# Whole 1 MB weight pieces split at once, from one pool of five tiles, and a narrow expert's product in three steps

## The chip, the cores and the metric

The kernel runs on one core of one Trainium2 chip. The metric is the device time of one execution in microseconds (us). TensorE is called PE, VectorE DVE, ScalarE ACT, GpSimd POOL and SyncE SP. An engine works through its own instructions in the order in which the program holds them, and waits where another engine's result, or a buffer, is not there yet.

## The reference

A trunk of two layers on 256 tokens of 1,024 channels, in float32:

```python
# layer 0: multi-head latent attention, then a dense SwiGLU of 3584 hidden channels
x = x + mla_mixer(rmsnorm(x, norm_mix[0]), ...)
h = rmsnorm(x, norm_ffn[0])
x = x + (silu(h @ ffn_w_gate) * (h @ ffn_w_up)) @ ffn_w_down
# layer 1: mLSTM, then the best 2 of 8 experts, each a SwiGLU of 3584 hidden channels
x = x + mlstm_mixer(rmsnorm(x, norm_mix[1]), ...)
h = rmsnorm(x, norm_ffn[1])
logits = h @ router; top_v, top_i = top_k(logits, 2); gates = softmax(top_v)
for e in range(8):
    y = y + combine[..., e:e+1] * ((silu(h @ wg[e]) * (h @ wu[e])) @ wd[e])
x = rmsnorm(x + y, final_norm)
```

The result must be as exact as float32. PE multiplies rounded numbers, so the kernel takes each weight as a sum of two rounded parts.

## The kernel before

**Weights.** They come by DMA from SP's queue in pieces of 1 MB, 128 partitions by 2,048 columns, into a pool of 10 slots (`raw`). `split` makes the two parts of a piece: ACT writes `whi`, the rounded copy (L204), and DVE writes `wlo`, what is left (L208). It does this in two halves of 1,024 columns, with four tiles for `whi` and four for `wlo`. A raw slot is free once DVE has read it, and a tile once PE has.

**FFN** (112 to 340 us). Seven chunks of 512 hidden channels, six pieces each: two of the gate, two of the up and two of the down weights.

**mLSTM** (340 to 460 us). `by_channel(0)` and `by_channel(1)` make queries and keys, two pieces each; `by_token` makes the values and the output gate. Between them stand small steps on DVE: the reciprocal root `mix1` (L378), the gates, and `convolved`, whose first step copies the query sums out of their PSUM bank times `rb` (`qks`, L898). `rb` comes out of `mix1`. PSUM has four banks with the tag "a": the two `by_channel` take all of them, and `by_token` gets its two when the `qks` of `by_channel(0)` have been done.

**Chores.** The router's logits are partly made by dot products of 1,024 columns on DVE (L768). They lie in the list `chores`: 64 of `out_dot` (8 rows of `mlstm_w_out` times 8 experts) and later 16 of `x_dot`. Each call of `split` takes one from the list and issues it ahead of its own split, from the third chunk of the FFN on. What is left when a stage ends is issued in one go:

```python
        if chores and begun[0]:
            chores.pop(0)()
...
    while chores:
        chores.pop(0)()
    aT = x_mix.pair
```

**Experts** (460 to 1436 us). Eight experts, each of seven chunks of six pieces. Wide and narrow ones alternate. A wide one has 128 slots for tokens, and a piece takes 12 matmuls of 512 columns there. A narrow one has 64, its two parts stand side by side in one operand, and a piece takes 8. In a narrow chunk `both_parts` turns the chunk's gate and up values by 16 small matmuls (L1307) and makes the product at once: ACT's silu (L1310), DVE's product (L1311), ACT's rounded part (L1312), DVE's rest (L1313). `Stream.run` sets the order: it keeps `AHEAD` halves split ahead of the one that PE takes, and `soon(n, f)` issues f after n more halves. The numbers `T_LAG`, `T_LAST` and `LAST` say how many halves `both_parts` waits and where the last expert's end begins.

Of the kernel before, what the change touches and what calls it, by code (L numbers as in the profile page):

```python
# [69 lines left out]
def trunk(ctx: ExitStack, tc: tile.TileContext, out, rope_inv, x, positions, norm_mix, norm_ffn,  # L70
# [71 lines left out]
    class Stream:  # L142
# [43 lines left out]

    def split(v, sub=nc.vector):
        vs = v if isinstance(v, list) else [v]
        shape = [P, 2, 512] if isinstance(v, list) else list(v.shape)
        n = int(np.prod(shape[1:]))  # L190
        hi = weights.tile([P, 1024], F32R, name=uniq("whi"), tag="whi", bufs=NB_HI)[:, :n]
        lo = weights.tile([P, 1024], F32R, name=uniq("wlo"), tag="wlo", bufs=NB_LO)[:, :n]
        if len(shape) == 3:
            hi = hi.rearrange("p (k c) -> p k c", k=shape[1])
            lo = lo.rearrange("p (k c) -> p k c", k=shape[1])
        if chores and begun[0]:
            chores.pop(0)()
        with ExitStack() as order:
            if held:
                for ins in held.pop(0):  # L200
                    order.enter_context(tc.issue_after(ins))
            for i, part in enumerate(vs):
                h, l = (hi[:, i], lo[:, i]) if isinstance(v, list) else (hi, lo)
# [236 lines left out]
    class Out:  # L440
# [6 lines left out]
        def weights(self, i):  # L447
            raw = load(self.w[i], [P, 2, D])
            return [split(raw[:, kk]) for kk in range(2)]

# [340 lines left out]
    class Chunk:  # L791


        def __init__(self, aT, r, nb, wg, wu, wd, c, down, before):
            self.nb, self.wd, self.c, self.down = nb, wd, c, down
            self.hid = []
            act = []
            for which, w in enumerate((wg, wu)):
                p = [ps("a", [P, 512]) for _ in range(nb)]
                for i in range(2):  # L800
                    raw = load(w[c, i], [P, 4, 512])
                    for k2 in range(2):
                        wp = split(raw[:, 2 * k2:2 * k2 + 2])
                        for b in range(nb):
                            k = 4 * i + 2 * k2
                            mm3s([(p[b], tok(aT, k + kk, b), at(wp, slice(None), kk), k + kk == 0, k + kk == KB - 1)
                                  for kk in range(2)])
# [24 lines left out]
        def finish(self, i):  # L832
            raw = load(self.wd[2 * self.c + i], [P, 2, D])
            self.down(self.c, i, self.parts, [split(raw[:, kk]) for kk in range(2)])

# [47 lines left out]
    def by_channel(piece):  # L883
        p2 = [ps("a", [P, 2, S]) for _ in range(2)]
        for i in range(2):
            raw = load(mlstm_w_in[piece, i], [P, 4, 512])
            for k2 in range(2):
                wp = split(raw[:, 2 * k2:2 * k2 + 2])
                for j in range(4):
                    for kk in range(2):  # L890
                        k = 4 * i + 2 * k2 + kk
# [79 lines left out]
    def by_token(c0):  # L971
        pv = [ps("a", [P, 512]) for _ in range(NT)]
        for i in range(2):
            raw = load(mlstm_w_in[c0 // 512, i], [P, 4, 512])
            for k2 in range(2):
                wp = split(raw[:, 2 * k2:2 * k2 + 2])
                for b in range(NT):
                    for kk in range(2):
                        k = 4 * i + 2 * k2 + kk
                        mm3(pv[b], tok(aT, k, b), at(wp, slice(None), kk), k == 0, k == KB - 1)  # L980
# [276 lines left out]

    def inner(e, i, p, j, w):
        if i + j == 0:
            p.append(ps("a", [P, 512]))  # L1260
        xg = tokens[e][0]
        k = 4 * i + 2 * j
        if not WIDE[e]:
            mm2s([(p[0], xg[:, k + kk], at(w, slice(None), kk), k + kk == 0, k + kk == KB - 1) for kk in range(2)])
            return
        mm3s([(p[0], (xg[:, 0, k + kk], xg[:, 1, k + kk]), at(w, slice(None), kk), k + kk == 0, k + kk == KB - 1)
              for kk in range(2)])

    def gated(e, c, p):
# [5 lines left out]
        if c == 3 and e + 1 < NE:  # L1275
# [18 lines left out]
    def upped(e, c, p):  # L1294
# [4 lines left out]
        else:  # L1299
            nc.scalar.copy(h, p[0])  # L1300

        def both_parts():

# [5 lines left out]
            hid = tmp([P, 2, 4, N], F32, "hT_lo")  # L1309
            nc.scalar.activation(hid[:, 0], t[:, 0], AF.Silu)  # L1310
            nc.vector.tensor_mul(hid[:, 1], t[:, 1], hid[:, 0])  # L1311
            nc.scalar.copy(pair[:, :, :N], hid[:, 1])  # L1312
            nc.vector.tensor_sub(pair[:, :, N:], hid[:, 1], pair[:, :, :N].bitcast(F32))  # L1313
            hT[e, c] = pair

        def transposed():
# [4 lines left out]
            lo = tmp([P, 4, P], F32R, "hT_lo")  # L1321
            nc.scalar.copy(hi, t)
            nc.vector.tensor_sub(lo, t, hi.bitcast(F32))
            hT[e, c] = hi, lo

        moe.soon(T_LAST if (e, c) == (NE - 1, NCH - 1) else T_LAG, transposed if WIDE[e] else both_parts)

# [4 lines left out]

    def outer(e, c, i, j, w):
        k = 2 * i + j
        for h in range(2):
            if c + k == 0:
                acc[h] = ps("b", [P, 512])
        if not WIDE[e]:
            mm2s([(acc[h], hT[e, c][:, k], at(w, slice(None), slice(h * 512, h * 512 + 512)),
                   c + k == 0, c == NCH - 1 and k == 3) for h in range(2)])  # L1340
            return
        mm3s([(acc[h], at(hT[e, c], slice(None), k), at(w, slice(None), slice(h * 512, h * 512 + 512)),
               c + k == 0, c == NCH - 1 and k == 3) for h in range(2)])

# [171 lines left out]
    gather(ohs[0], first_parts, 1)  # L1516
    moe.fill(4)
    their_weights()
# [114 lines left out]
```

## Time and profile before

| | |
|---|---|
| median of 3 runs | 1442.95 us (1442.86 to 1444.77) |
| profiled execution | 1442.82 us, of which the span from the first to the last instruction is 1441.1 us |
| PE busy | 1384.9 us (96%) |
| DVE busy | 1255.8 us (87%) |
| ACT busy | 997.6 us (69%) |
| mean granted clock of PE | 0.993 of full speed |

All times are counted from the span's start. The profiled execution has 1.7 us around its span. A busy PE may be a PE that goes slowly, since matmuls are pipelined and the ends of their records are modelled; so a stage's limit is read from its waits and from the time of one chunk.

### The profile page before, as it was taken

The page shows a single profiled execution, that of the slowest core. Times are in us where ns is not written, and L with a number is a line of the kernel's source. Part 1 is how long each engine was busy: PE and PEld are TensorE (multiplying, and loading weights), DVE is VectorE, ACT ScalarE, POOL GpSimd, SP SyncE. Part 2 cuts the span into 40 slices and gives each one's busy share as a digit, 9 for nine tenths or more (in the row PEclk, how much of TensorE's full clock was granted, in tenths as well). Part 3 has the DMA queues.
Part 4 walks back from the last instruction along what each step waited for, and adds up shares of the span by engine and source line. Part 5 has one row for each costly group of instructions (what it writes and reads, how often), then busy time and mean ns, then how long its engine had stood idle before and what let it go on. Part 6 is the DMA issues. An engine that isn't in the chain of part 4 may idle for free.

```text
span 1441.1 us, 18851 instructions
## 1 busy us (share of the span) xinstructions
PE 1384.9 (96%) x6457; PEld 1080.9 (75%) x6457; DVE 1255.8 (87%) x1604; ACT 997.6 (69%) x1272; POOL 51.4 (4%) x99
## 2 busy tenths in 40 slices
PE   7999999999999899999999999999999999999995
PEld 5888888888777688766688877678886667887663
DVE  6869998857987988999998898998899899889996
ACT  5544444445854777878877788877777887778885
POOL 4300000000031000000000000000000000000000
PEclk9999999999999999999999999999999999999998
DMA  9456656555557868899999999999999999999990
GB/s 360 154 203 220 216 194 227 193 177 206 204 201 287 290 234 339 326 380 368 407 354 335 360 365 363 395 406 361 334 375 357 364 404 371 341 376 352 384 370 32
DMA packets 63614, 439.06 MB, mean 305 GB/s; under 512 B 7489, under 2 KB 7654, under 8 KB 11798
## 3 DMA queue, kind: packets, MB, share of 16 engines
q1 hardware_dynamic: 61478, 428.15, 78.5%
q0 software_dynamic: 1872, 9.61, 1.8%
q8 instruction: 52, 0.85, 0.2%
q14 instruction: 52, 0.43, 0.1%
q10 hardware_dynamic: 160, 0.02, 0.0%
HBM read 436.67 MB, written 1.08 MB: 304 GB/s over the span
## 4 chain that ended last, share of the span: by engine, by line
PE 81%; DVE 10%; issue 3%; ACT 3%; POOL 1%; DMA 0%; ACTq 0%; DVEq 0%; POOLq 0%
PE ps_a L220 10%; PE ps_a L221 10%; PE ps_a L223 10%; PE ps_a L230 8%; DVE wlo L208 6%; PE ps_a L228 6%; PE ps_b L230 4%; PE ps_b L220 3%; PE ps_b L223 3%; PE ps_b L221 3%; PE ps_a L1307 3%; PE ps_b L228 3%; PE ps_b L215 3%; PE ps_b L213 3%; PE ps_b L214 3%
## 5 line engine op out<-in xcount | busy, mean ns | idle before, releaser
L208 DVE TENSOR_TENSOR wlo<-raw,whi 128x1024 fp32r<-128x1024 f32 (+1 forms) x783 | 914.5, 1218 | 99.1 <-ACT whi L204 97.6
L204 ACT CAST whi<-raw 128x1024 fp32r<-128x1024 f32 (+1 forms) x792 | 793.2, 1048 | 200.4 <-PE ps_a L221 107.6
L220 PE MATMUL ps_a<-whi,xg 128*128 128x512 f32 x448 | 177.0, 395 | 1.1 <-ACT whi L204 1.1
L221 PE MATMUL ps_a<-whi,xg 128*128 128x512 f32 x448 | 176.5, 394 | 0.0
L230 PE MATMUL ps_a<-wlo,xg 128*128 128x512 f32 x448 | 156.1, 430 | 12.2 <-DVE wlo L208 12.2
L228 PE MATMUL ps_a<-whi,xg 128*128 128x512 f32 x448 | 142.2, 399 | 0.0
L223 PE MATMUL ps_a<-wlo,xg 128*128 128x512 f32 x448 | 140.3, 394 | 1.9 <-DVE wlo L208 1.9
L230 PEld LDWEIGHTS ps_a<-wlo,xg 128*128 128x128 f32 x448 | 72.1, 188 | 76.4 <-DVE wlo L208 70.3
L223 PEld LDWEIGHTS ps_a<-wlo,xg 128*128 128x128 f32 x448 | 83.8, 188 | 22.7 <-DVE wlo L208 3.2
L220 PEld LDWEIGHTS ps_a<-whi,xg 128*128 128x128 f32 x448 | 84.2, 188 | 20.8 <-ACT whi L204 1.5
L228 PEld LDWEIGHTS ps_a<-whi,xg 128*128 128x128 f32 x448 | 82.7, 188 | 22.5 <-ACT whi L204 4.5
L221 PEld LDWEIGHTS ps_a<-whi,xg 128*128 128x128 f32 x448 | 84.2, 188 | 19.8 <-DVE xg L1500 0.5
L220 PE MATMUL ps_b<-whi,hT_hi 128*128 128x512 f32 x224 | 91.2, 407 | 0.0
L220 PE MATMUL ps_a<-whi,xT_hi 128*128 128x512 f32 x224 | 88.6, 395 | 0.1
L221 PE MATMUL ps_a<-whi,xT_lo 128*128 128x512 f32 x224 | 88.4, 394 | 0.0
L221 PE MATMUL ps_b<-whi,hT_lo 128*128 128x512 f32 x224 | 88.3, 394 | 0.0
L768 DVE CUSTOM_DVE_ANT_0 junk<-raw,wr 128x1024 bf16<-128x1024 f32 x64 | 78.0, 1219 | 2.1 <-DMA raw<-mlstm_w_out_dram 1.6
L230 PE MATMUL ps_b<-wlo,hT_hi 128*128 128x512 f32 x224 | 76.3, 420 | 0.5 <-DVE wlo L208 0.5
L228 PE MATMUL ps_b<-whi,hT_hi 128*128 128x512 f32 x224 | 73.9, 409 | 1.0 <-ACT whi L204 1.0
L223 PE MATMUL ps_b<-wlo,hT_hi 128*128 128x512 f32 x224 | 70.3, 395 | 0.0
L223 PE MATMUL ps_a<-wlo,xT_hi 128*128 128x512 f32 x224 | 70.0, 393 | 0.0
L213 PE MATMUL ps_b<-whi,hT_hi 128*128 128x512 f32 x152 | 60.9, 401 | 0.0
(443 smaller groups left out, 1883.0 us busy)
## 6 DMA issues: line engine op xcount, KB each, us to landing
raw<-moe_w_gate_dram SPq DMA_DIRECT2D x112, 1024.0 KB, 7.1
raw<-moe_w_up_dram SPq DMA_DIRECT2D x112, 1024.0 KB, 7.0
raw<-moe_w_down_dram SPq DMA_DIRECT2D x105, 1024.0 KB, 7.3
raw<-ffn_w_gate_dram SPq DMA_DIRECT2D x14, 1024.0 KB, 5.0
raw<-ffn_w_up_dram SPq DMA_DIRECT2D x14, 1024.0 KB, 4.8
raw<-ffn_w_down_dram SPq DMA_DIRECT2D x14, 1024.0 KB, 4.8
raw<-mlstm_w_in_dram SPq DMA_DIRECT2D x12, 1024.0 KB, 5.1
raw<-mla_w_out_dram SPq DMA_DIRECT2D x4, 1024.0 KB, 7.7
```

What stands on the lines that cost most here:

```text
L204: nc.scalar.copy(h, part)
L208: sub.tensor_sub(l, part, h.bitcast(F32))
L213: nc.tensor.matmul(o, l[0], r[0], start=start, stop=False)
L214: nc.tensor.matmul(o, l[0], r[1], start=False, stop=False)
L215: nc.tensor.matmul(o, l[1], r[0], start=False, stop=stop)
L220: nc.tensor.matmul(o, l[0], r[0], start=start, stop=False)
L221: nc.tensor.matmul(o, l[1], r[0], start=False, stop=False)
L223: nc.tensor.matmul(o, l[0], r[1], start=False, stop=stop)
L228: nc.tensor.matmul(o, l, r[0], start=start, stop=False)
L230: nc.tensor.matmul(o, l, r[1], start=False, stop=stop)
L768: nc.vector.tensor_tensor_reduce(junk, a, b, 1.0, 0.0, OP.mult, OP.add, acc)
L1307: nc.tensor.matmul(t[:, n, j], src[:, j * P:(j + 1) * P], twice, start=n + j == 0, stop=n + j == 4)
```

## The change

A piece is split whole: one ACT copy and one subtraction on DVE of 2,048 columns each. Both parts come from one pool, "part", of five tiles of 2,048 columns; a split of up to 1,024 columns keeps both parts in one such tile, and the gates' weights of the mLSTM (`wg`) take a tile of it too. There are nine raw slots. `soon`, `AHEAD`, `LAST` and `T_LAG` count pieces now. The product of a narrow expert comes in three steps, one piece apart: the small matmuls, then silu and product, then the two parts. The cast and the rest of a wide expert come a piece behind their transposes. One early `fill` at the start of the experts is left out. `split` itself still takes one chore per call, but there is one call per piece where there were two.

```diff
-NB_RAW = 10
-NB_HI = 4
-NB_LO = 4
-AHEAD = 3
+NB_RAW = 9
+NB_PART = 5
+AHEAD = 2
...
-LAST = 10
-T_LAG = 2
-T_LAST = 1
+LAST = 7
+T_LAG = 1
...
-            self.items.append((partial(get, 0), lambda w: use(0, w), None))
-            self.items.append((partial(get, 1), lambda w: use(1, w), after))
+            self.items.append((lambda sub: split(load(None if key in early else src(), shape, key), sub), use, after))
...
-        hi = weights.tile([P, 1024], F32R, name=uniq("whi"), tag="whi", bufs=NB_HI)[:, :n]
-        lo = weights.tile([P, 1024], F32R, name=uniq("wlo"), tag="wlo", bufs=NB_LO)[:, :n]
+        if n <= 1024:
+            t = weights.tile([P, 2048], F32R, name=uniq("whl"), tag="part", bufs=NB_PART)
+            hi, lo = t[:, :n], t[:, 1024:1024 + n]
+        else:
+            hi, lo = (weights.tile([P, 2048], F32R, name=uniq(name), tag="part", bufs=NB_PART) for name in ("whi", "wlo"))
...
         if chores and begun[0]:
             chores.pop(0)()
...
                     raw = load(w[c, i], [P, 4, 512])
-                    for k2 in range(2):
-                        wp = split(raw[:, 2 * k2:2 * k2 + 2])
...
+                    wp = split(raw)
...
-    wg = weights.tile([P, KB, 2, 2 * HEADS], F32R, name=uniq("whi"), tag="whi", bufs=NB_HI)
+    wg = weights.tile([P, KB, 2, 2 * HEADS], F32R, name=uniq("wg"), tag="part", bufs=NB_PART)
...
+        at_end = (e, c) == (NE - 1, NCH - 1)
+
+        def then(f):
+
+            f() if at_end else moe.soon(1, f)
+
...
-            nc.scalar.activation(hid[:, 0], t[:, 0], AF.Silu)
-            nc.vector.tensor_mul(hid[:, 1], t[:, 1], hid[:, 0])
-            nc.scalar.copy(pair[:, :, :N], hid[:, 1])
-            nc.vector.tensor_sub(pair[:, :, N:], hid[:, 1], pair[:, :, :N].bitcast(F32))
...
+            def product():
+                nc.scalar.activation(hid[:, 0], t[:, 0], AF.Silu)
+                nc.vector.tensor_mul(hid[:, 1], t[:, 1], hid[:, 0])
+                then(parts)
+
+            def parts():
+                nc.scalar.copy(pair[:, :, :N], hid[:, 1])
+                nc.vector.tensor_sub(pair[:, :, N:], hid[:, 1], pair[:, :, :N].bitcast(F32))
+
+            then(product)
...
-    moe.fill(3, PUT_OFF)
...
-    moe.fill(4)
+    moe.fill(3)
```

The first place is DVE in a narrow expert's chunk. Before, two halves of the split, the product (L1311), the rest of its parts (L1313), and two halves again:

```order
L208 TENSOR_TENSOR wlo_1762_7604<-raw_1757_7591,whi_1761_7603 128x1024
L208 TENSOR_TENSOR wlo_1767_7616<-raw_1765_7613,whi_1766_7615 128x1024
L1311 TENSOR_TENSOR hT_lo_1770_7633<-ps_a_1768_7623,hT_lo_1770_7633 128x256
L1313 TENSOR_TENSOR hT_hi_1769_7632<-hT_lo_1770_7633,hT_hi_1769_7632 128x4x64
L208 TENSOR_TENSOR wlo_1772_7639<-raw_1765_7613,whi_1771_7638 128x1024
L208 TENSOR_TENSOR wlo_1775_7649<-raw_1773_7646,whi_1774_7648 128x1024
```

Now, from the same place of a chunk on, the split being L198 and the rest of the parts L1316:

```order
L198 TENSOR_TENSOR wlo_1367_6839<-raw_1365_6836,whi_1366_6838 128x2048
L1311 TENSOR_TENSOR hT_lo_1364_6835<-ps_a_1362_6825,hT_lo_1364_6835 128x256
L198 TENSOR_TENSOR wlo_1370_6855<-raw_1368_6852,whi_1369_6854 128x2048
L1316 TENSOR_TENSOR hT_hi_1363_6834<-hT_lo_1364_6835,hT_hi_1363_6834 128x4x64
L198 TENSOR_TENSOR wlo_1374_6872<-raw_1372_6869,whi_1373_6871 128x2048
```

The product and the rest of its parts no longer follow each other; a whole split stands between them, and one ahead of each.

The second place is DVE behind the FFN. Before, it holds the steps of `mix1` (L378), halves of the splits for `by_channel`, and one `x_dot` (L768, with the row that reads its sum):

```order
L378 TENSOR_SCALAR mix1_v_632_3056<-turned_s_614_2926 128x2
L768 ISA junk_673_3300,x_wr_1076<-xs_75,raw_672_3298 128x1024
L768 ISA x_wr_1076 128x1
L208 TENSOR_TENSOR wlo_631_3029<-raw_627_2998,whi_630_3028 128x1024
L378 TENSOR_SCALAR mix1_y_633_3057<-mix1_v_632_3056 128x2
L208 TENSOR_TENSOR wlo_658_3174<-raw_656_3171,whi_657_3173 128x1024
L378 TENSOR_SCALAR mix1_y_633_3057<-mix1_y_633_3057 128x2
L378 TENSOR_SCALAR mix1_v_632_3056<-mix1_v_632_3056 128x2
L208 TENSOR_TENSOR wlo_660_3202<-raw_656_3171,whi_659_3201 128x1024
```

Now, behind the split of the first piece of `by_channel(1)` (`wlo_552`), each step of `mix1` (L368) stands behind an `out_dot` (L759, `wo_wr`):

```order
L198 TENSOR_TENSOR wlo_552_2972<-raw_550_2969,whi_551_2971 128x2048
L759 ISA junk_480_2668,wo_wr_1049<-raw_479_2666,wr_199_1041 128x1024
L759 ISA wo_wr_1049 128x1
L368 TENSOR_SCALAR mix1_v_526_2854<-turned_s_476_2660 128x2
L759 ISA junk_481_2670,wo_wr_1049<-raw_479_2666,wr_199_1041 128x1024
L759 ISA wo_wr_1049 128x1
L368 TENSOR_SCALAR mix1_y_527_2855<-mix1_v_526_2854 128x2
L759 ISA junk_482_2672,wo_wr_1049<-raw_479_2666,wr_200_1043 128x1024
L759 ISA wo_wr_1049 128x1
L368 TENSOR_SCALAR mix1_y_527_2855<-mix1_y_527_2855 128x2
L368 TENSOR_SCALAR mix1_v_526_2854<-mix1_v_526_2854 128x2
L759 ISA junk_483_2674,wo_wr_1049<-raw_479_2666,wr_200_1043 128x1024
```

The list had 64 `out_dot`, and 32 calls of `split` are left for them in the FFN (six in each of five chunks, and two behind). The other 32 stand here, one by one between the steps of `mix1`, the gates, the last split for `by_channel(1)`, and the first of `convolved` (L893). Behind them come the third and fourth `qks` and the first split for `by_token`.

## Rows read from the trace of the kernel before

**Rows 1.** The page: span, busy time of each engine, chain that ended last

```profile
span 1441.1 us, 18851 instructions
PE 1384.9 (96%) x6457; PEld 1080.9 (75%) x6457; DVE 1255.8 (87%) x1604; ACT 997.6 (69%) x1272; POOL 51.4 (4%) x99
...
PE 81%; DVE 10%; issue 3%; ACT 3%; POOL 1%; DMA 0%; ACTq 0%; DVEq 0%; POOLq 0%
```

**Rows 2.** Busy time by stretch; columns as in its first row

```profile
core 0: us, PE busy (x) PEld busy (x) DVE busy (x) ACT busy (x) POOL busy (x), PEclk, DMA share, GB/s
112.00:340.00 228.00, 227.94 (x1021) 185.76 (x1020) 187.57 (x244) 98.36 (x111) 1.56 (x4) 1.00 0.58 205
340.00:460.00 120.00, 117.56 (x667) 97.04 (x666) 101.27 (x224) 78.09 (x144) 12.27 (x21) 1.00 0.61 223
691.31:706.80 15.49, 15.49 (x71) 11.59 (x71) 14.49 (x16) 13.16 (x17) 0.00 (x0) 1.00 0.98 401
792.20:809.40 17.20, 17.20 (x78) 13.87 (x77) 15.31 (x15) 13.23 (x15) 0.00 (x0) 1.00 1.00 362
940.00:960.00 20.00, 19.10 (x84) 14.90 (x83) 19.00 (x20) 17.50 (x22) 0.00 (x0) 1.00 1.01 421
```

**Rows 3.** Waits by line, 601 to 709 us: total, times, longest

```profile
PEld ps_a L230 <- DVE wlo L208: 16.8, 36, 1.1
```

**Rows 4.** Chain that ended last, 690 to 706 us: start, us, what

```profile
697.78 1.73 PE ps_a L1307 x16
```

**Rows 5.** Timeline of DVE there; in brackets the idle time before

```profile
686.70 13.71 DVE L208 TENSOR_TENSOR wlo<-raw,whi 128x1024 fp32r<-128x1024 f32 x12 [0.53 <-ACT whi L204]
700.34 0.41 DVE L1311 TENSOR_TENSOR hT_lo<-ps_a,hT_lo 128x256 f32<-128x256 f32 x1
701.22 0.42 DVE L1313 TENSOR_TENSOR hT_hi<-hT_lo,hT_hi 128x256 fp32r<-128x256 f32 x1 [0.47 <-ACT hT_hi L1312]
702.17 1.23 DVE L208 TENSOR_TENSOR wlo<-raw,whi 128x1024 fp32r<-128x1024 f32 x1 [0.52 <-ACT whi L204]
```

**Rows 6.** Timeline of ACT there

```profile
685.62 5.78 ACT L204 CAST whi<-raw 128x1024 fp32r<-128x1024 f32 x6
```

**Rows 7.** DVE splits by shape: ns min/median/max, first and last start

```profile
L208 DVE TENSOR_TENSOR wlo<-raw,whi x783: 1083/1217/1229, 12.6 to 1419.5; 128x1024 fp32r<-128x1024 f32 x195, 128x896 fp32r<-128x896 f32 x1
L208 DVE TENSOR_TENSOR wlo<-tables,whi x2: 683/684/684, 505.9 to 1420.7; 128x512 fp32r<-128x512 f32 x2
```

**Rows 8.** ACT splits by shape, same columns

```profile
L204 ACT CAST whi<-raw x792: 817/1050/1070, 11.2 to 1418.3; 128x1024 fp32r<-128x1024 f32 x195, 128x768 fp32r<-128x768 f32 x2, 128x896 fp32r<-128x896 f32 x1
L204 ACT CAST whi<-tables x2: 613/616/619, 504.6 to 1419.2; 128x512 fp32r<-128x512 f32 x2
```

**Rows 9.** Dots of the router by shape, same columns

```profile
L768 DVE CUSTOM_DVE_ANT_0 junk<-raw,wr x64: 1209/1218/1228, 111.0 to 326.5; 128x1024 bf16<-128x1024 f32 x64
L768 DVE CUSTOM_DVE_ANT_0 junk<-xs,raw x16: 1210/1218/1240, 346.4 to 425.6; 128x1024 bf16<-128x1024 f32 x16
```

**Rows 10.** Timeline of DVE behind the FFN

```profile
346.37 1.22 DVE L768 CUSTOM_DVE_ANT_0 junk<-xs,raw 128x1024 bf16<-128x1024 f32 x1
347.51 1.22 DVE L208 TENSOR_TENSOR wlo<-raw,whi 128x1024 fp32r<-128x1024 f32 x1
...
364.21 0.42 DVE L898 TENSOR_TENSOR qks<-ps_a,rb 128x256 f32<-128x256 f32 x1
365.68 1.22 DVE L768 CUSTOM_DVE_ANT_0 junk<-xs,raw 128x1024 bf16<-128x1024 f32 x1
```

**Rows 11.** Timeline of PE: first matmuls of by_channel and of by_token

```profile
339.55 0.39 PE L213 MATMUL ps_a<-xT_hi,whi 128*128 128x256 f32 x1
...
366.28 0.40 PE L213 MATMUL ps_a<-whi,xT_hi 128*128 128x512 f32 x1
```

**Rows 12.** Busy time in parts of the mLSTM stage; columns as in rows 2

```profile
347.00:366.00 19.00, 19.00 (x158) 18.48 (x157) 18.58 (x47) 11.91 (x17) 0.00 (x0) 1.00 0.61 223
366.00:421.00 55.00, 54.54 (x267) 42.79 (x266) 45.92 (x99) 42.20 (x89) 9.60 (x15) 1.00 0.48 170
```

More of the change, by code (lines that the diff above doesn't have):

```diff
@@ L188, in split @@
         vs = v if isinstance(v, list) else [v]
-        shape = [P, 2, 512] if isinstance(v, list) else list(v.shape)
+        shape = [P, 2, D] if isinstance(v, list) else list(v.shape)
         n = int(np.prod(shape[1:]))
-        hi = weights.tile([P, 1024], F32R, name=uniq("whi"), tag="whi", bufs=NB_HI)[:, :n]
-        lo = weights.tile([P, 1024], F32R, name=uniq("wlo"), tag="wlo", bufs=NB_LO)[:, :n]
+        if n <= 1024:
[3 more added lines that the diff above has]
+            hi, lo = (weights.tile([P, 2048], F32R, name=uniq(name), tag="part", bufs=NB_PART) for name in ("whi", "wlo"))
         if len(shape) == 3:
-            hi = hi.rearrange("p (k c) -> p k c", k=shape[1])
-            lo = lo.rearrange("p (k c) -> p k c", k=shape[1])
+            hi, lo = (part.rearrange("p (k c) -> p k c", k=shape[1]) for part in (hi, lo))
         if chores and begun[0]:
@@ L202, in split @@
             for i, part in enumerate(vs):
-                h, l = (hi[:, i], lo[:, i]) if isinstance(v, list) else (hi, lo)
+                h, l = [t[:, i // 2, i % 2 * 512:(i % 2 + 1) * 512] if isinstance(v, list) else t for t in (hi, lo)]
                 nc.scalar.copy(h, part)
@@ L448, in weights @@
             raw = load(self.w[i], [P, 2, D])
-            return [split(raw[:, kk]) for kk in range(2)]
+            wp = split(raw)
+            return [at(wp, slice(None), kk) for kk in range(2)]
         def rows(self, i, pair, wps=None, between={}):
@@ L801, in __init__ @@
                     raw = load(w[c, i], [P, 4, 512])
-                    for k2 in range(2):
-                        wp = split(raw[:, 2 * k2:2 * k2 + 2])
[L804 to L807, printed above, removed]
+                    wp = split(raw)
+                    for b in range(nb):
+                        k = 4 * i
+                        mm3s([(p[b], tok(aT, k + kk, b), at(wp, slice(None), kk), k + kk == 0, k + kk == KB - 1)
+                              for kk in range(4)])
                 for b in range(nb):
@@ L833, in finish @@
             raw = load(self.wd[2 * self.c + i], [P, 2, D])
-            self.down(self.c, i, self.parts, [split(raw[:, kk]) for kk in range(2)])
+            wp = split(raw)
+            self.down(self.c, i, self.parts, [at(wp, slice(None), kk) for kk in range(2)])
     aT = x_ffn.pair
@@ L886, in by_channel @@
             raw = load(mlstm_w_in[piece, i], [P, 4, 512])
+            wp = split(raw)
             for k2 in range(2):
-                wp = split(raw[:, 2 * k2:2 * k2 + 2])
                 for j in range(4):
-                    for kk in range(2):
-                        k = 4 * i + 2 * k2 + kk
+                    for kk in range(2 * k2, 2 * k2 + 2):
+                        k = 4 * i + kk
                         mm3(p2[j // 2][:, j % 2], at(wp, slice(None), kk, slice(j * P, (j + 1) * P)),
@@ L974, in by_token @@
             raw = load(mlstm_w_in[c0 // 512, i], [P, 4, 512])
+            wp = split(raw)
             for k2 in range(2):
-                wp = split(raw[:, 2 * k2:2 * k2 + 2])
                 for b in range(NT):
-                    for kk in range(2):
-                        k = 4 * i + 2 * k2 + kk
+                    for kk in range(2 * k2, 2 * k2 + 2):
+                        k = 4 * i + kk
                         mm3(pv[b], tok(aT, k, b), at(wp, slice(None), kk), k == 0, k == KB - 1)
@@ L1256, in expert_chunk, with inner @@
                           partial(after, e, c, p) if i else None)
-    def inner(e, i, p, j, w):
-        if i + j == 0:
+    def inner(e, i, p, w):
+        if i == 0:
             p.append(ps("a", [P, 512]))
         xg = tokens[e][0]
-        k = 4 * i + 2 * j
+        k = 4 * i
         if not WIDE[e]:
-            mm2s([(p[0], xg[:, k + kk], at(w, slice(None), kk), k + kk == 0, k + kk == KB - 1) for kk in range(2)])
+            mm2s([(p[0], xg[:, k + kk], at(w, slice(None), kk), k + kk == 0, k + kk == KB - 1) for kk in range(4)])
             return
         mm3s([(p[0], (xg[:, 0, k + kk], xg[:, 1, k + kk]), at(w, slice(None), kk), k + kk == 0, k + kk == KB - 1)
-              for kk in range(2)])
+              for kk in range(4)])
     def gated(e, c, p):
@@ L1321, in transposed, with parts @@
             lo = tmp([P, 4, P], F32R, "hT_lo")
-            nc.scalar.copy(hi, t)
-            nc.vector.tensor_sub(lo, t, hi.bitcast(F32))
             hT[e, c] = hi, lo
-        moe.soon(T_LAST if (e, c) == (NE - 1, NCH - 1) else T_LAG, transposed if WIDE[e] else both_parts)
+            def parts():
+                nc.scalar.copy(hi, t)
+                nc.vector.tensor_sub(lo, t, hi.bitcast(F32))
+            then(parts)
+        moe.soon(T_LAG, transposed if WIDE[e] else both_parts)
     def expert_down(e, c):
@@ L1331, in expert_down, with outer @@
                       partial(summed, e) if i and c == NCH - 1 else None, (e, c, i))
[L1333 to L1336, printed above, removed]
+    def outer(e, c, i, w):
+        if c + i == 0:
+            for h in range(2):
                 acc[h] = ps("b", [P, 512])
[L1338 to L1343, printed above, removed]
+        (mm3s if WIDE[e] else mm2s)(
+            [(acc[h], at(hT[e, c], slice(None), 2 * i + kk) if WIDE[e] else hT[e, c][:, 2 * i + kk],
+              at(w, slice(None), kk, slice(h * 512, h * 512 + 512)), c + i + kk == 0, c == NCH - 1 and i + kk == 2)
+             for kk in range(2) for h in range(2)])
     def summed(e):
```

20 lines of the change are left out of this document (6 added, 14 removed).

## The prediction

> **What bounds the kernel now.** I began with the page: PE is busy 96% of the span, DVE 87%, and the chain that ended last runs 81% on PE and 10% on DVE [rows 1]. Such shares mix stages, so the next view is the busy time by stretch [rows 2]. In the FFN PE is busy 227.94 of 228.00 us, in a wide expert's chunk 17.20 of 17.20, and DVE has room in both: these are bound by PE. In a narrow expert's chunk (691.31 to 706.80 us) PE shows 15.49 of 15.49, but DVE stands at 14.49 too. Which of them it is, the waits tell: in the first narrow expert the weight loads of L230, those that need `wlo`, wait 16.8 us for DVE, 36 times [rows 3]. The timeline of DVE shows a chunk as a closed loop [rows 5]: twelve halves in 13.71 us, L1311, a gap of 0.47, L1313, a gap of 0.52, and the next twelve begin at 702.17, 15.47 us after the first began at 686.70. So the narrow experts go at DVE's pace. PE's own work in a chunk is less: a wide chunk does 72 matmuls of 512 columns in 17.20 us, so one takes at most 0.239; 48 of them and the 16 small ones (1.73 us, [rows 4]) are 13.2 us.
>
> The mLSTM stage, which the change touches by its chores, has no cover: between 347 and 366 us PE is busy 19.00 of 19.00 and DVE 18.58 [rows 12]. PE comes to `by_token`'s first matmul at 366.28 [rows 11], right after the fourth `qks` on DVE at 364.21 and a split that ends at 365.68 [rows 10].
>
> **The narrow chunk after.** A split of 512 columns takes 0.683 us on DVE and one of 1,024 takes 1.217 [rows 7], that is 0.534 for 512 columns more; so I estimate 2.285 for 2,048. Back to back, twelve halves take 13.71, so each starts (13.71 - 1.217)/11 = 1.136 after the one before, 0.081 before that has ended. A whole piece then takes 2.285 - 0.081 = 2.204, against 2.272 for two halves: 0.07 saved, 0.41 a chunk. The larger part is the two gaps: L1313 waits for ACT's rounded part, and the split behind it for ACT's next `whi`, since ACT itself waited for L1311. In the new order a whole split stands between L1311 and L1316, so ACT has 2.2 us for a cast that held DVE up for 0.47, and both gaps (0.99) close. The chunk is 6 x 2.204 + 0.41 + 0.42 = 14.05 us, 1.42 less than 15.47. Seven chunks in three experts and six in the last, whose end is done at once, make 27 x 1.42 = 38 us. That is one bound.
>
> **What else a narrow chunk needs.** ACT: 512 columns take 0.616 and 1,024 take 1.050 [rows 8]; six in a row take 5.78 [rows 6], so (5.78 - 1.05)/5 = 0.946 each. A whole piece is by the same step 1.050 + 2 x 0.434 - 0.104 = 1.81. ACT was busy 13.16 us in a chunk [rows 2], of which twelve halves are 11.35 and the rest 1.81; six whole pieces and that rest are 12.7: under 14.05, but a `whi` must find a tile of the five free, and PE holds tiles longer while its 1.73 us of small matmuls stand ahead of a piece. DMA: six pieces are 6.29 MB, which in 14.05 us would be 448 GB/s. No stretch shows that: the fullest one moves 421 with all DMA engines busy (share 1.01) [rows 2]. At 421 a chunk lasts 14.94. Pieces that have landed ahead bridge it: the shortfall is 0.89 us of transfer a chunk, 0.36 piece, 2.5 pieces over seven chunks, and a wide expert at 17.20 us a chunk leaves the time to fill the nine slots again (6.29 MB there need 366 GB/s). If the reserve is never there, the saving is 0.53 x 27 = 14 us, the other bound. I take 30: two to three pieces of reserve out of nine slots are likely, some loss to ACT and tiles is too.
>
> The Trainium skill, "DMA: Bandwidth & Descriptors", section "Where 436 GB/s comes from", says that for transfers from HBM to SBUF a limit of about 358 GB/s for a core binds, below the fabric's 435. By that rule a narrow chunk would need 17.6 us and the term would be nothing. The trace disagrees: that chunk moved 401 GB/s [rows 2], and I give the rule no chance.
>
> **The chores.** Here the change takes away a cover. Each `split` hides one `out_dot`; with half as many calls only 32 of 64 run in the FFN. Before, all 64 began before 326.5 us [rows 9], under a PE that was the bound, and cost nothing. The order puts the other 32 on DVE behind `wlo_552`, ahead of the third and fourth `qks` and of the first split of `by_token`. One costs 1.14 us: the dot at 346.37 is followed by the next large operation at 347.51 [rows 10]. 32 x 1.14 = 36.5. What is queued behind them: the steps of `mix1`, the gates, `qks`, and PE's `by_token`, which needs the banks that the `qks` free, and its `wlo`. PE has only the two pieces of `by_channel(1)` to do meanwhile. The walk: before, 346.37 to 365.68 held four `x_dot` (4.6) and seven halves (8.0), so some 6.7 of small steps. After, five tiles with one taken by `wg` let `wlo_552` end about 351: PE must first have done one of the four pieces of `by_channel`, which take it from 339.55 to 366.28 [rows 11], 6.7 each, so to 346.2, and then ACT and DVE take some 2 us each. Then 36.5 + 6.7, one whole split of 2.2, one `x_dot` of 1.1 and the split of `by_token`, 2.2: DVE is done about 400, and PE goes on there instead of at 366.28, less the overlap of its first matmuls: 34. Bounds: later DVE has slack, 45.92 busy of 55.00 [rows 12], which could win 9 back (25); the gaps of each small step behind a dot could add 5 (39). I take 34, as PE itself was busy 54.54 of those 55.00 and can't catch up. Of the 16 `x_dot`, twelve are left to the end of `by_token`; most lie beside its products: 1 (0 to 4).
>
> **What costs or brings nothing.** Whole pieces in the FFN and the wide experts save DVE 0.4 us a chunk, hidden behind PE; without that cover it would be 7 + 28 chunks x 0.4, 14 us. The cast of a wide expert one piece later lies beside 2.8 us of matmuls. Nine slots for ten and the `fill` that is left out matter only where a load is late, which the DMA bound above holds. Where PE starts from nothing, the first `wlo` of a stage comes 2.285 - 1.217 = 1.07 later: two or three such places (attention, FFN, mLSTM or experts): 2 (0 to 4).
>
> **Sum**, against the profiled 1442.82 (0.13 below the median of the runs): -30 + 34 + 1 + 2 = +7, so **1450 us**, 0.5% slower. By the bounds alone: -38 + 25 to -14 + 39 + 8, from 1430 to 1476. What a measurement here can't tell from no change is 0.2%, 2.9 us.
>
> **Rivals.**
> *The chores find cover* (ends faster). If DVE wins back the 9 us of slack and the narrow experts give all of 38, the time is 1443 - 38 + 25 + 1 = 1431. For it: DVE's slack after 366. Against: PE has no more slack there than 0.46 of 55. It decides once the chores cost less than the narrow experts give.
> *Narrow experts go at the pace of DMA*: 14.94 a chunk, -14, so 1466. For it: share 1.01 at 421 GB/s already now. Against: those stretches may only refill slots.
> *The three steps don't close the gaps*: ACT's whole copy of 1.9 us stands where L1311 or the rounded part has to be, each late by a copy, and tiles are short. Then only 0.41 x 27 = 11 us are saved, or nothing: 1469 to 1480. Against: ACT has 1.4 us a chunk to spare.
> *The change doesn't do what it says*: the order shows both that pieces are whole and that chores are left, so I give this nothing.
>
> **How the numbers follow.** Forecast (1440 to 1458) 0.53; cover found (1422 to 1440) 0.20; DMA's pace (1458 to 1468) 0.19; gaps stay (above 1468) 0.08. The range from 1431 to 1468 leaves out half of the second case and all of the last, 0.18. Faster by over 0.2% (below 1440) is the second case and a little of the forecast's lower end, 0.22; within 0.2% (1440 to 1446) takes a quarter of the forecast, 0.15; slower 0.63.
>
> **What the profile after should show.** DVE: L198 at 2.29 us, a chunk of about 14.1 to 14.5 us in narrow experts, no idle time before L1316, and under 16.8 us of waits for `wlo` there. Behind the FFN: 32 dots of L759 between about 351 and 398, PE idle for over 30 us ahead of `by_token`, and the first expert starting later by as much. Wide chunks stay at 17.2 us. The prediction is wrong if PE is not idle there, or if DMA's share is 1.0 all through a narrow expert with `whi` waiting for `raw`.

## The result, and the profile after

The changed kernel takes 1455.88 us (median of four runs), the kernel before beside it 1443.86: by these two medians a ratio of 1.0083. The ratio worked out over the single runs is 1.0095, with a 95% interval from 1.0082 to 1.0107. It is slower by 12.0 us; 1450 had been forecast, 6 to 7 us above the kernel before. The profiled executions, with spans of 1453.9 and 1441.1 us, show where that comes from.

The page first: its span, the engines, PE's granted clock over the 40 slices, and the chain that ended last.

```profile
span 1453.9 us, 17916 instructions
PE 1362.9 (94%) x6457; PEld 1101.8 (76%) x6457; DVE 1222.8 (84%) x1209; ACT 953.2 (66%) x877; POOL 54.1 (4%) x99
...
PEclk9999999999689999999999999999999999999998
...
PE 53%; DVE 10%; issue 1%; ACT 1%; DVEq 0%; ACTq 0%
```

PE, DVE and ACT are each busy for less time than before [rows 1], and the span is longer all the same. The new thing is in the clock's row: two slices, from about 363 to 436 us, stand at 6 and 8 tenths.

Busy time by stretch (columns as in rows 2): the FFN, a plain chunk of the first narrow expert, a wide chunk, two stretches behind the FFN, and one behind the heads.

```profile
112.00:340.00 228.00, 227.60 (x1027) 186.25 (x1026) 149.21 (x145) 92.35 (x73) 1.09 (x2) 1.00 0.54 188
669.20:683.10 13.90, 13.40 (x66) 10.57 (x64) 13.90 (x10) 12.59 (x12) 0.00 (x0) 1.00 1.00 411
780.40:797.60 17.20, 17.20 (x77) 13.91 (x77) 14.77 (x9) 12.54 (x8) 0.00 (x0) 1.00 0.98 353
380.00:400.00 20.00, 2.08 (x6) 0.82 (x6) 19.85 (x44) 3.92 (x7) 0.61 (x2) 0.52 0.30 102
400.00:408.00 8.00, 6.00 (x13) 4.42 (x14) 8.00 (x12) 4.84 (x5) 0.00 (x0) 0.50 0.41 140
470.00:480.00 10.00, 7.12 (x24) 4.64 (x25) 10.00 (x20) 5.00 (x5) 0.53 (x1) 0.83 1.02 428
```

The narrow chunk now takes 13.90 us, DVE busy all through; 14.05 was forecast. The FFN (227.60 of 228.00) and the wide chunk (17.20 of 17.20) are PE's, as before. But from 380 to 400 us PE is busy 2.08 of 20, and when it starts again its granted clock is 0.50.

DVE's timeline over that narrow chunk:

```profile
669.14 0.42 DVE L1316 TENSOR_TENSOR hT_hi<-hT_lo,hT_hi 128x256 fp32r<-128x256 f32 x1
669.48 11.09 DVE L198 TENSOR_TENSOR wlo<-raw,whi 128x2048 fp32r<-128x2048 f32 x5
680.49 0.42 DVE L1311 TENSOR_TENSOR hT_lo<-ps_a,hT_lo 128x256 f32<-128x256 f32 x1
680.83 2.29 DVE L198 TENSOR_TENSOR wlo<-raw,whi 128x2048 fp32r<-128x2048 f32 x1
683.04 0.42 DVE L1316 TENSOR_TENSOR hT_hi<-hT_lo,hT_hi 128x256 fp32r<-128x256 f32 x1
```

Five whole pieces in 11.09 us, L1311, one piece, L1316, and the next, with no idle time in between: the two gaps of [rows 5] are gone. The waits of that expert (637 to 745 us) say the same; they show besides that ACT now waits for a tile that PE still reads:

```profile
ACT whi L194 <- PE ps_b L220: 8.3, 7, 1.5
PEld ps_a L220 <- DVE wlo L198: 5.6, 11, 0.9
```

The weight loads for `ps_a` wait 5.6 us for `wlo`, where it was 16.8 [rows 3].

Behind the FFN, DVE's timeline, the first and the last of the 32 dots, the fourth `qks`, and the first split of `by_token`:

```profile
349.28 1.22 DVE L759 CUSTOM_DVE_ANT_0 junk<-raw,wr 128x1024 bf16<-128x1024 f32 x1
...
394.88 1.22 DVE L759 CUSTOM_DVE_ANT_0 junk<-raw,wr 128x1024 bf16<-128x1024 f32 x1
...
399.74 0.41 DVE L889 TENSOR_TENSOR qks<-ps_a,rb 128x256 f32<-128x256 f32 x1
400.07 0.47 DVE L893 SCALAR_TENSOR_TENSOR conv<-qks,col,conv 128x254 f32<-128x254 f32 x1
400.46 2.28 DVE L198 TENSOR_TENSOR wlo<-raw,whi 128x2048 fp32r<-128x2048 f32 x1
```

And PE at `by_token`:

```profile
378.48 0.47 PE L203 MATMUL ps_a<-whi,xT_hi 128*128 128x512 f32 x1 [2.91 <-DVE qks L889]
...
400.21 0.79 PE L203 MATMUL ps_a<-whi,xT_hi 128*128 128x512 f32 x1 [8.97 <-DVE qks L889]
402.80 0.79 PE L204 MATMUL ps_a<-wlo,xT_hi 128*128 128x512 f32 x1 [1.80 <-DVE wlo L198]
...
404.24 0.63 PE L204 MATMUL ps_a<-wlo,xT_hi 128*128 128x512 f32 x1
404.67 0.63 PE L205 MATMUL ps_a<-whi,xT_lo 128*128 128x512 f32 x1
...
408.08 0.40 PE L205 MATMUL ps_a<-whi,xT_lo 128*128 128x512 f32 x1
408.31 0.39 PE L203 MATMUL ps_a<-whi,xT_hi 128*128 128x512 f32 x1
```

One matmul of `by_token` runs at 378.48, in the bank that the second `qks` has freed. Then PE waits for the fourth `qks`, which frees the other bank, and for `wlo`, and goes on at 402.80; before, `by_token` began at 366.28 and ran on [rows 11]. From 403.39 the matmuls start 0.43 apart; from 408 on they are 0.23 apart.

Five stretches between six points tell how the difference of 12.8 us in the span came together. The points are the starts of PE's 1,481st, 1,801st, 2,041st and 2,101st instruction, and of the instruction with which ACT takes a chunk's gate sums:

| point | before | after | later by |
|---|---|---|---|
| late in the FFN | 328.23 | 326.88 | -1.4 |
| in the first product of `by_token` | 377.21 | 413.22 | +36.0 |
| near the end of the output gate's product | 426.79 | 464.71 | +37.9 |
| output projection of the mLSTM | 440.17 | 483.59 | +43.4 |
| gate of expert 0, second chunk | 485.8 | 532.5 | +46.7 |
| gate of the last expert, last chunk | 1407.3 | 1419.7 | +12.3 |

37.4 us are lost between the FFN and `by_token`, 1.9 in the heads, 5.5 behind them, and 3.3 up to the second chunk of the first expert. From there to the last chunk the experts win back 34.4: the narrow ones 29.6, the wide ones 4.8.

### The profile page after: what moved, and what is told of

It is laid out like the page before. It is cut to its first block, busy times and chain, and to the rows that moved or that the text cites. A ratio compares the mean times of both kernels' runs of the same rounds, so it can differ in the third digit from the quotient of the medians.

```text
span 1453.9 us, 17916 instructions
## 1 busy us (share of the span) xinstructions
PE 1362.9 (94%) x6457; PEld 1101.8 (76%) x6457; DVE 1222.8 (84%) x1209; ACT 953.2 (66%) x877; POOL 54.1 (4%) x99
## 4 chain that ended last, share of the span: by engine, by line
PE 53%; DVE 10%; issue 1%; ACT 1%; DVEq 0%; ACTq 0%
DVE wlo L198 8%; PE ps_a L210 7%; PE ps_a L211 7%; PE ps_a L213 7%; PE ps_a L218 5%; PE ps_a L220 4%; PE ps_b L220 4%; PE ps_b L210 4%; PE ps_b L211 4%; PE ps_b L213 3%; PE ps_a L1304 3%; PE ps_b L218 2%; PE ps_a L1496 2%; PE ps_b L1430 1%; PE ps_a L1323 1%
## 5 line engine op out<-in xcount | busy, mean ns | idle before, releaser
L198 DVE TENSOR_TENSOR wlo<-raw,whi 128x2048 fp32r<-128x2048 f32 x390 | 883.2, 2290 | 156.6 <-ACT whi L194 70.1
L194 ACT CAST whi<-raw 128x2048 fp32r<-128x2048 f32 x391 | 743.2, 1912 | 244.7 <-PE ps_a L213 112.6
L210 PE MATMUL ps_a<-whi,xg 128*128 128x512 f32 x448 | 177.5, 396 | 0.6 <-ACT whi L194 0.6
L211 PE MATMUL ps_a<-whi,xg 128*128 128x512 f32 x448 | 176.5, 394 | 0.1
L220 PE MATMUL ps_a<-wlo,xg 128*128 128x512 f32 x448 | 125.0, 400 | 7.3 <-DVE wlo L198 6.9
L213 PE MATMUL ps_a<-wlo,xg 128*128 128x512 f32 x448 | 121.4, 393 | 1.7 <-DVE wlo L198 1.5
L218 PE MATMUL ps_a<-whi,xg 128*128 128x512 f32 x448 | 121.8, 393 | 0.0
L220 PEld LDWEIGHTS ps_a<-wlo,xg 128*128 128x128 f32 x448 | 81.0, 188 | 37.0 <-DVE wlo L198 20.6
L213 PEld LDWEIGHTS ps_a<-wlo,xg 128*128 128x128 f32 x448 | 84.0, 188 | 21.3 <-DVE wlo L198 1.9
L210 PE MATMUL ps_b<-whi,hT_hi 128*128 128x512 f32 x224 | 91.2, 407 | 0.0
L211 PE MATMUL ps_b<-whi,hT_lo 128*128 128x512 f32 x224 | 88.3, 394 | 0.0
L759 DVE CUSTOM_DVE_ANT_0 junk<-raw,wr 128x1024 bf16<-128x1024 f32 x64 | 78.1, 1220 | 0.6
L220 PE MATMUL ps_b<-wlo,hT_hi 128*128 128x512 f32 x220 | 63.2, 409 | 6.9 <-DVE wlo L198 5.6
L218 PE MATMUL ps_b<-whi,hT_hi 128*128 128x512 f32 x220 | 63.2, 409 | 2.2 <-DVE hT_hi L1316 2.2
L204 PE MATMUL ps_b<-wlo,hT_hi 128*128 128x512 f32 x152 | 60.9, 401 | 1.0 <-DVE wlo L198 1.0
L213 PE MATMUL ps_b<-wlo,hT_hi 128*128 128x512 f32 x224 | 61.2, 395 | 0.0
L205 PE MATMUL ps_b<-whi,hT_lo 128*128 128x512 f32 x152 | 60.9, 401 | 0.0
```

The lines of the kernel that those rows point to most:

```text
L204: nc.tensor.matmul(o, l[0], r[1], start=False, stop=False)
L205: nc.tensor.matmul(o, l[1], r[0], start=False, stop=stop)
L210: nc.tensor.matmul(o, l[0], r[0], start=start, stop=False)
L211: nc.tensor.matmul(o, l[1], r[0], start=False, stop=False)
L213: nc.tensor.matmul(o, l[0], r[1], start=False, stop=stop)
L218: nc.tensor.matmul(o, l, r[0], start=start, stop=False)
```

## The experiments

Ratios are those of the runs beside the kernel before on the same chip; it took 1442.85 to 1443.09 us there. Its single runs lie between 1441.2 and 1445.5 us, so differences of 1 or 2 us between experiments say little.

**Two chores a whole piece.** Theory A says that the chores lost their cover. Theory B says that whole pieces and the five shared tiles make `by_token` late, and that the dots only fill a wait.

```diff
-        if chores and begun[0]:
-            chores.pop(0)()
+        for _ in range(2 if n > 1024 else 1):
+            if chores and begun[0]:
+                chores.pop(0)()
```

> The changed kernel, but each split of a whole piece takes two chores, so that all 64 dots of the router's weights run under the FFN again and the 16 others under by_token. Theory A (the chores lost their cover): by_token's first matmul goes back from 400.2 us to about 366, the products after the head no longer wait for y, and of the 12.8 us lost some 44 come back: about 1411 us, faster than the kernel before by 32. Theory B (whole pieces and the pool of five tiles, one held by the gates' weights, make by_token late, and the dots only fill a wait that would be there anyway): PE still waits over 20 us ahead of by_token, and the time stays above 1435 us.

1419.06 us, ratio 0.9828 (0.9812 to 0.9845): 36.8 us less than the changed kernel. PE's first matmul of `by_token` in its timeline:

```profile
366.09 0.40 PE L204 MATMUL ps_a<-whi,xT_hi 128*128 128x512 f32 x1
```

It is back where it was, and the next ones follow it without a wait. Theory B falls for the wait ahead of `by_token`. But 1411 us were expected, and 8 are missing; the trace is ahead by 1 us at `by_token`, behind by 1.8 at the end of its products, by 5.9 at the output projection, and by 10.2 at the second chunk of the first expert. Something else than the number of chores costs there.

**Half the chores in the kernel before.** The complement: halves and their eight tiles stay, and only every second call of `split` takes a chore.

```diff
-        if chores and begun[0]:
+        calls[0] += begun[0]
+        if chores and begun[0] and calls[0] % 2:
             chores.pop(0)()
```

> The kernel before, but only every second half of a split takes a chore, so 32 dots are left for the time behind the FFN, as in the changed kernel; all else is as before. Theory A: PE waits some 35 to 37 us ahead of by_token and 5 behind the head, and the time is 1443 + 42 to 45 = about 1486 us. Theory B: the halves and the four tiles let by_token's split be made between the dots, and the time grows by less than 20 us, below 1463.

1476.83 us, 1.0230 (1.0213 to 1.0248): 33.7 more than the kernel before. PE's timeline, the first matmul of `by_token` and the first that needs its `wlo`:

```profile
395.07 0.79 PE L215 MATMUL ps_a<-whi,xT_hi 128*128 128x512 f32 x1 [2.58 <-DVE qks L900]
...
401.70 0.51 PE L216 MATMUL ps_a<-wlo,xT_hi 128*128 128x512 f32 x1 [0.63 <-DVE wlo L210]
```

The first starts when the `qks` frees its bank, the other when its `wlo` is there, at 401.70; the point that the table has at 377.21 us stands at 410.27, 33.1 later. So the lost cover alone, without a whole piece anywhere, costs 33 to 34. The time is 9 us short of the 1486 expected: at the second chunk of the first expert this kernel is 35.5 us behind the kernel before, and the changed one 46.7. What the changed kernel loses beyond the dots is not in this one.

**One step again.** The changed kernel with the narrow product at once.

```diff
-                then(parts)
+                parts()
...
-            then(product)
+            product()
```

> The changed kernel with the narrow product in one step again: silu, product, cast and rest follow the small matmuls at once, one piece after the chunk, with whole pieces. Theory C (the three steps close two gaps of DVE of together 1 us a chunk, and most of the 33 us won in the experts is theirs): the gaps come back, larger since ACT's copy of 1.9 us can stand between the steps, a plain narrow chunk takes 15 to 16 us instead of 13.9, and the time is 1456 + 27 to 45 = 1483 to 1500 us. Theory D (whole pieces alone win it): the chunk stays within 0.3 us of 13.9 and the time below 1465 us.

1500.78 us, 1.0394 (1.0376 to 1.0411), 44.9 above the changed kernel. DVE's timeline of a chunk:

```profile
669.32 13.30 DVE L198 TENSOR_TENSOR wlo<-raw,whi 128x2048 fp32r<-128x2048 f32 x6 [1.38 <-ACT whi L194]
682.54 0.42 DVE L1311 TENSOR_TENSOR hT_lo<-ps_a,hT_lo 128x256 f32<-128x256 f32 x1
683.43 0.43 DVE L1316 TENSOR_TENSOR hT_hi<-hT_lo,hT_hi 128x256 fp32r<-128x256 f32 x1 [0.47 <-ACT hT_hi L1315]
685.24 6.70 DVE L198 TENSOR_TENSOR wlo<-raw,whi 128x2048 fp32r<-128x2048 f32 x3 [1.39 <-ACT whi L194]
```

The chunk takes 15.92 us, longer than before the change: behind L1311 come gaps of 0.47 and of 1.39, since ACT makes the next `whi` only behind the rounded part, and a whole one takes it 1.9 us. Whole pieces without the three steps would have made the narrow experts slower than they were. Theory D falls.

**Three steps alone.** The kernel before with the same steps, two halves apart.

```diff
+            def then(f):
+
+                f() if (e, c) == (NE - 1, NCH - 1) else moe.soon(2, f)
+
+            def product():
                 nc.scalar.activation(hid[:, 0], t[:, 0], AF.Silu)
                 nc.vector.tensor_mul(hid[:, 1], t[:, 1], hid[:, 0])
+                then(parts)
+
+            def parts():
                 nc.scalar.copy(pair[:, :, :N], hid[:, 1])
                 nc.vector.tensor_sub(pair[:, :, N:], hid[:, 1], pair[:, :, :N].bitcast(F32))
+
+            then(product)
```

> The kernel before with the narrow product in three steps, two halves apart; halves, tiles and chores are as before. Theory C: both gaps close, a plain chunk takes 12 x 1.136 + 0.83 = 14.5 us instead of 15.47, and 27 chunks give 26 us: about 1417 us. Theory D: nothing, 1443 us.

1415.70 us, 0.9808 (0.9791 to 0.9824). DVE's timeline:

```profile
670.14 0.42 DVE L1323 TENSOR_TENSOR hT_hi<-hT_lo,hT_hi 128x256 fp32r<-128x256 f32 x1
670.48 11.44 DVE L208 TENSOR_TENSOR wlo<-raw,whi 128x1024 fp32r<-128x1024 f32 x10
681.84 0.41 DVE L1318 TENSOR_TENSOR hT_lo<-ps_a,hT_lo 128x256 f32<-128x256 f32 x1
682.17 2.35 DVE L208 TENSOR_TENSOR wlo<-raw,whi 128x1024 fp32r<-128x1024 f32 x2
684.44 0.42 DVE L1323 TENSOR_TENSOR hT_hi<-hT_lo,hT_hi 128x256 fp32r<-128x256 f32 x1
```

No gaps, and a chunk of 14.30 us. Theory C holds: 27.4 us come from closing two gaps, by an edit that touches neither pieces, tiles nor chores.

**The dots of the FFN alone.** Two chores a split in the FFN, one in the mLSTM.

```diff
-        if chores and begun[0]:
-            chores.pop(0)()
+        for _ in range(2 if n > 1024 and not wr_done else 1):
+            if chores and begun[0]:
+                chores.pop(0)()
...
+    wr_done.append(True)
     aT = x_mix.pair
```

> The changed kernel with two chores a split in the FFN only: the 64 dots with mlstm_w_out run there again, the 16 with x go one a split as in the change. If the dots in front of by_token are what costs, some 35 of the 36.8 us that two chores everywhere gave back come back here: 1456 - 35 = about 1421 us. If the dots with x behind the head cost much by themselves (they stand one by one between the steps of y), it is 1424 to 1427.

1423.20 us, 0.9861 (0.9845 to 0.9877). 32.7 us come back with the 32 dots, and 4.1 more (to 1419.06) with two chores in the mLSTM too: between the two outcomes, nearer to the second. Of the 16 dots with x, 12 run behind the heads in the changed kernel and in this one, and 8 in the kernel before and with two chores everywhere; so four dots cost the 4.1. In the changed kernel, DVE's timeline shows how:

```profile
465.26 0.08 DVE L759 DVE_READ_ACCUMULATOR2_ANT x_wr<- 128x1 f32 x1
465.53 1.22 DVE L759 CUSTOM_DVE_ANT_0 junk<-xs,raw 128x1024 bf16<-128x1024 f32 x1
...
466.67 0.35 DVE L1226 SCALAR_TENSOR_TENSOR y<-wts,head_y,og 128x128 f32<-128x128 f32 x1
466.94 1.22 DVE L759 CUSTOM_DVE_ANT_0 junk<-xs,raw 128x1024 bf16<-128x1024 f32 x1
```

The first steps of `y` each stand behind a dot, and PE's transposes wait for `y` one by one:

```profile
468.58 0.30 PE L1228 MATMUL ps_a<-ident,y 128*128 128x128 f32 x1 [0.93 <-DVE y L1226]
469.89 0.33 PE L1228 MATMUL ps_a<-ident,y 128*128 128x128 f32 x1 [1.02 <-DVE y L1226]
```

**Halves outside the experts.** What are the 8 us? Here, with two chores a whole piece, the mLSTM's weights and both output projections are in halves again; FFN and experts keep whole pieces.

```diff
-            wp = split(raw)
-            return [at(wp, slice(None), kk) for kk in range(2)]
+            return [split(raw[:, kk]) for kk in range(2)]
...
-            wp = split(raw)
             for k2 in range(2):
+                wp = split(raw[:, 2 * k2:2 * k2 + 2])
```

> Two chores a whole split, but the mLSTM's weights and both output projections are split in halves again (one chore each, both parts of a half in one tile of the five); FFN and experts keep whole pieces. Two chores everywhere left the first expert 6 us behind the kernel before at its start, and 10 at its second chunk. If whole pieces in the mLSTM stage cost the 6 (a later first rest, another order of the head's products), they come back: about 1413 us. If the five shared tiles do, it stays at 1419.

1411.05 us, 0.9777 (0.9761 to 0.9793): 8.0 less than with whole pieces there, a little more than the expected 6. Compared with the three steps alone (1415.70), whole pieces in the experts and the FFN, with the pool, the slots and the later cast that came with them, are worth 4.7 us.

**Its two parts.** The mLSTM's weights alone, and the projections alone, in halves.

> Two chores a whole split; only the mLSTM's input weights (by_channel and by_token) are in halves with one chore each; the two output projections keep whole pieces, as do FFN and experts. With both in halves the time was 8.0 us below that with neither (1411.05 to 1419.06). If by_token's whole pieces cost the most of it (with them the reciprocal root of the heads began 6 us later against its own products, and y with it), 1413 to 1415 us. If the projections do, 1416 to 1418.

1411.68 us, 0.9790 (0.9774 to 0.9806): less still than the 1413 to 1415 expected if these weights cost the most.

> The complement: only the output projections of attention and mLSTM in halves, the mLSTM's input weights whole with two chores. If by_token's pieces cost the most, 1416 to 1418 us; if the projections do, 1413 to 1415. The two parts should add up to about 8.

1415.56 us, 0.9815 (0.9799 to 0.9832). That is between the two outcomes. The mLSTM's weights give 7.4 of the 8.0; the projections give 3.5 by themselves, and almost nothing beside the others, so the two overlap and don't add up to 8 as expected. A piece of the way can be seen in DVE's timelines, at the start of the heads' reciprocal root and at the first `y`. The kernel before:

```profile
409.78 0.17 DVE L364 TENSOR_SCALAR head_v<-hsq 128x16 f32<-128x16 f32 x1 [0.18 <-POOL hsq L1037]
...
421.65 0.35 DVE L1235 SCALAR_TENSOR_TENSOR y<-wts,head_y,og 128x128 f32<-128x128 f32 x1 [2.30 <-POOL head_y L1039]
```

Two chores, all whole:

```profile
418.05 0.18 DVE L355 TENSOR_SCALAR head_v<-hsq 128x16 f32<-128x16 f32 x1 [0.18 <-POOL hsq L1029]
...
427.64 0.35 DVE L1227 SCALAR_TENSOR_TENSOR y<-wts,head_y,og 128x128 f32<-128x128 f32 x1 [3.57 <-POOL head_y L1031]
```

The changed kernel:

```profile
449.13 0.17 DVE L354 TENSOR_SCALAR head_v<-hsq 128x16 f32<-128x16 f32 x1 [0.18 <-POOL hsq L1028]
...
462.44 0.35 DVE L1226 SCALAR_TENSOR_TENSOR y<-wts,head_y,og 128x128 f32<-128x128 f32 x1 [2.59 <-POOL head_y L1030]
```

Two chores, the mLSTM in halves:

```profile
407.80 0.17 DVE L355 TENSOR_SCALAR head_v<-hsq 128x16 f32<-128x16 f32 x1 [0.18 <-POOL hsq L1029]
...
419.73 0.35 DVE L1227 SCALAR_TENSOR_TENSOR y<-wts,head_y,og 128x128 f32<-128x128 f32 x1 [2.31 <-POOL head_y L1031]
```

With two chores and whole pieces the root begins 8.3 us later than before and `y` 6.0 later; with halves both are 2 us earlier than before. PE's order moved with the pieces. The values and the output gate take 192 matmuls of 512 columns in `by_token`, 96 each. Ahead of the heads' last products, which feed the root, the traces have 97 of them before, 98 with the mLSTM in halves, 104 in the changed kernel and 125 with two chores and all whole: there 28 matmuls of the gate, at 0.234 us 6.6 us, went ahead of what `y` waits for. In the changed kernel, with 104, the root is 39.4 us later than before, some 3 more than the 36.0 of `by_token`.

**Six tiles.** Two chores, all whole, eight slots and six tiles.

> Two chores a split, and eight raw slots and six tiles in place of nine and five (the same memory). If the tiles bind whole pieces (ACT waits for a tile while PE still reads), the starts of the experts and the narrow chunks after the first (16.4 us) get shorter: 1410 to 1415 us. If the slots bind (a reserve of landed pieces for the narrow experts at 448 GB/s), narrow chunks get longer than 13.9, towards 14.9: 1425 to 1440. If neither binds, 1419.

1416.49 us, 0.9812 (0.9796 to 0.9828). That is between 1419 and the 1410 to 1415 that were expected if the tiles bind. From the first expert's second chunk to the last expert's last it takes 883.7 us, with five tiles 889.4: in the experts the tiles bind whole pieces a little, and the slots don't. The second chunk of the first expert starts at 497.5 us here and at 496.1 with five tiles, so a sixth tile does not bring back what halves outside the experts do.

**The sixth tile with halves outside.** Slots and tiles as eight and six, and as seven and seven, on top of halves outside the experts.

> Halves outside the experts and FFN, two chores a whole split, and eight raw slots with six tiles. From the first expert's second chunk to the last's, six tiles took 883.6 us where five took 889.3 and 889.1. If the two gains add up, 1411.0 - 5.5 = about 1405.5 us. If the sixth tile only shifts waits to the loads, 1409 to 1412.

1410.54 us, 0.9773 (0.9757 to 0.9789). The experts are 5 us shorter here too (883.9 for 889.1), but PE is already 4.6 us later at the end of the FFN; the sum is that of nine and five. The expected 1405.5 did not come, and why PE is late there was not followed up.

> The same with seven raw slots and seven tiles. With a load of 7 us from issue to landing and a piece every 2.3 us in a narrow expert, seven slots, two of them being split, leave about five under way or landed, enough for the pace of 13.9 us only if the transfers run without a break. If the reserve of landed pieces matters, narrow chunks lengthen towards 14.9 and the time is 1412 to 1430 us; if it doesn't, 1403 to 1406.

1411.33 us, 0.9780 (0.9764 to 0.9797). Even with seven slots a narrow chunk keeps its pace (columns as in rows 2):

```profile
628.90:642.80 13.90, 13.41 (x66) 10.59 (x64) 13.90 (x10) 12.52 (x12) 0.00 (x0) 1.00 0.99 414
```

The reserve of landed pieces suffices; the rival of DMA's pace is out. The time is still above the 1403 to 1406 that were expected with it; PE is 3.7 us later at the end of the FFN than with nine and five. These two and the one with nine slots can't be told apart; all are some 32 us faster than the kernel before and 45 faster than the changed one.

## Why the prediction was wrong

The direction was right, the time lay inside the range, and the mechanisms of the two large terms came: the dots lost their cover and the narrow experts' gaps closed. The slowdown was mis-sized, since both small terms were too small. Term by term, by the medians of the experiments:

- **The dots ahead of `by_token`**: 34 forecast (25 to 39); 32.7 by undoing them, 33.7 by making them alone, 37.4 in the trace of the changed kernel. The walk said that DVE is done with the first split of `by_token` about 400; it was at 402.7.
- **The narrow experts**: -30 forecast (-14 to -38). With halves outside and two chores, what is left of the change gives -32.0, and in the trace of the changed kernel the narrow experts give 29.6. The size was right, but not for the main reason that brought it from 38 down to 30: the reserve of landed pieces sufficed, even with seven slots. A plain chunk gained more than forecast (13.90 for 14.05); an expert's second chunk gained nothing (16.38 us, before 16.22), the one with the next expert's gather 0.7 (18.68, before 19.42) and the last 0.4 (15.32, before 15.76), so an expert gave 7.3 us and not 9.9. That the sum came out so near is in part luck. The wide ones gave about 1 each, where nothing was forecast; which edit they owe it to was not tested.
- **"Where PE starts from nothing, the first `wlo` of a stage comes ... 1.07 later ... 2 (0 to 4)"**: this is the step that failed. Whole pieces outside the experts and the FFN cost 8.0, outside its bounds. I had counted late first splits alone; the runs show that the larger part lies in the mLSTM's weights (7.4), where the order of PE's products moved with the pieces and the heads' root began later. The 8.0 was taken with two chores, where that order is another than in the changed kernel (125 for 104); undone in another order, the edits might share the sum otherwise.
- **The dots with x, "most lie beside its products: 1 (0 to 4)"**: 4.1. Four more of them than before stand behind the heads, between the steps of `y`, on which PE waits.

The last two are 12.1 for 3, an error of 9.1; the dots and the experts together came out 3.3 better than forecast, which hid a third of it. 9.1 - 3.3 is the 5.8 between +7 and the 12.8 that these four steps add up to.

Of the profile, L198 at 2.29 us, no idle time ahead of L1316, and PE's idle time ahead of `by_token` came as expected. The plain narrow chunk was shorter than the 14.1 to 14.5 expected, and the first expert's gate came 44.6 us later where about 34 was expected. Of the rivals, the chores found no cover, DMA did not set the pace, and the gaps closed. How much of the 8.0 is the order of the products, how much the coarser first split, and how much that a half gives its tile back sooner, was not separated.

## What to carry to other kernels

A list of small jobs that is worked off "one per call" hangs on the number of calls: whoever makes pieces twice as large halves the cover, and the rest lands at once, on an engine that others wait for. A loop between two engines (DVE, ACT, DVE) is opened by putting one unit of other work between its steps; here that was worth 27 us without any larger piece, and larger pieces without it made the same loop slower (15.92 us a chunk for 15.47). Around the mLSTM halves were 7 to 8 us faster than whole pieces, and only a part of the way is shown; in the long steady loops of the FFN and the experts whole pieces, with what came with them, were worth some 5 us.

## What the runs showed of the hardware

PE's granted clock was 0.52 from 380 to 400 us, with PE busy 2.08 of 20 us, and 0.50 from 400 to 408, when it worked again: 1.2 of 2.4 GHz. Thirteen products from 402.80 to 408.31 started some 0.43 apart; at 0.234 they would have taken 3.0 us and not 5.5. So by these rows the long wait cost, as an estimate, 2.5 us more than its length, which I had not put in. The Trainium skill, "TensorE: Matmul & The Clock Gate", Part 1, says that the array's clock is throttled by default and that activity releases the throttle. The trace agrees: from 408.3 to 420 us, with PE busy all the time, the granted clock was 1.00.

A whole split took 2.291 us on DVE (median), for 2.285 estimated from two shorter ones, and starts 2.2 apart: six in a row took 13.30 us (in the run with one step again) and twelve halves 13.71 [rows 5], 0.4 us a chunk.
